# A seventh row pair in seven products, its sums T loaded apart for the first and last pair, and two low halves per block on GpSimd

## The chip, the cores and the metric

The kernel runs on one core of a Trainium2 chip. The core has a matrix engine (TensorE, PE in the profile), a vector engine (VectorE, DVE), a scalar engine (ScalarE, ACT), GpSimd (POOL) and SyncE (SP), which here only issues DMAs. The engines have queues of their own and meet at semaphores; matrix products land in PSUM, in eight banks of 128 x 512 fp32. The metric is the device time of one execution, in microseconds (us).

## The reference

Two pre-norm residual layers over 256 tokens of width 2048, each a token mixer (HGRN2 in layer 0, gated linear attention in layer 1) beside a cross-attention into 256 memory tokens, an output projection, and a SwiGLU feed-forward block with 5632 hidden columns. Everything is in fp32. The change is in the feed-forward part of both layers:

```python
hn = _rmsnorm(h, norm_ffn[layer])
gate, up = jnp.split(hn @ w_gate_up[layer], 2, axis=-1)
h = h + (jax.nn.silu(gate) * up) @ w_down[layer]
```

with `hn` of 256 x 2048, `w_gate_up` of 2048 x 11264 and `w_down` of 5632 x 2048.

## The kernel before

**Split factors.** A product of fp32 matrices is made as three matmuls of fp32r operands: each factor is split into a high part (a copy rounded to fp32r, by ACT) and a low part (the factor less its high part, by DVE), and high x high, high x low and low x high are summed in one PSUM bank. The low part of the weights is called the low half below; `split` makes both parts for one tile of raw weights.

**Blocks.** `ffn` goes over 11 blocks of 512 hidden columns. `up_block(b)` makes the 256 x 512 gate and up columns of block b with `project_halves`; a block reads 16 row tiles of 128 rows, taken as eight row pairs p = 0 to 7. Each pair has a 2 x 2 structure: two halves of the tokens by two row tiles on the left, two row tiles by two column groups (c0 for gate, c1 for up) on the right. There are three ways to make it, a letter for each pair in `KINDS`:

- S, seven products: the seven-product scheme for 2 x 2 matrices, in `seven`. It needs left forms s, d0, u, z and four combinations of the raw weights on the right, one of them T, the sum of the two row tiles in columns c1.
- O, eight products from the raw weights.
- H, eight products from the raw weights with one more difference of them (e1).

The string "SSOSSOSS", the last of `KINDS`, holds for blocks 4 to 10. The products go into seven PSUM banks, numbered 1 to 7, summed over the eight pairs; `TIMES` counts them.

**Raw weights.** `load_pair` loads the four tiles of a pair into one of three raw buffers (128 x 4 x 512) through SP's queue. For an S pair in the feed-forward part (`fed`), T is made by DMAs: SP loads the first row tile's c1 columns into place 1 of the raw buffer, and GpSimd issues a DMA that adds the second row tile's onto it. The second must wait for the first to land. The buffer is free when the last instruction that reads it is done. The split parts go into tiles a, b, c and d of the pair (`parts354c` is part c of the 354th raw tile); the larger ones share six buffers.

**Order.** From block 0's pair 3 on the order on PE, DVE and ACT is the program's (`Engine.kept`); GpSimd's and SP's are the scheduler's. Between the up blocks two pieces of the down projection run (`down`, tiles fd), each with one or two loads of 512 down weight rows (`weights`, two splits each). Work that belongs to block b but is done later is put down with a due key (`due`) and runs where `mark` passes it (`WHEN`): the sums of the seven banks (`sums`, tiles e and s), the gate (`gate`), the transposes (`turn`), and the copy of the finished down sums to h (`give_back`). From block 1 on the sums run right after the first down weights are split, and from block 3 on the copies to h run at the end of the second down load and at the second pair of the next block.

**The low half on GpSimd.** DVE's sums read one operand from PSUM. `sums` puts the name of its first addition into `free_port`; the next `split` takes it out, gives its low half to GpSimd, and makes it wait for that addition.

**Left forms.** `h_forms` makes the left factors of all pairs ahead of the block, eight forms for an S pair and six for an O pair (`Forms`, `PAIRS`).

Of the kernel before, what the change touches and what calls it, by code (L numbers as in the profile page):

```python
# [9 lines left out]
F32 = mybir.dt.float32  # L10
F32R = mybir.dt.float32r
BF16 = mybir.dt.bfloat16
U8 = mybir.dt.uint8
AF = mybir.ActivationFunctionType
ALU = mybir.AluOpType
AX = mybir.AxisListType

P = 128
T = 256
# [7 lines left out]
DFF = 5632  # L27
# [13 lines left out]
def trunk_kernel(ctx: ExitStack, tc: tile.TileContext, x, mem, norm_mix, norm_ffn, norm_mem,  # L41
                 norm_final, hgrn_w_in, hgrn_lb_logits, hgrn_onorm, gla_w_in, gla_w_gk,
                 gla_b_gk, gla_onorm, w_mem_kv, w_out, w_gate_up, w_down, c_ident, c_mask, out):
    nc = tc.nc

    const = ctx.enter_context(tc.tile_pool(name="const", bufs=1))
    wts = ctx.enter_context(tc.tile_pool(name="wts", bufs=1))
    away = ctx.enter_context(tc.tile_pool(name="away", bufs=1, space=bass.MemoryType.DRAM))
    opp = ctx.enter_context(tc.tile_pool(name="opp", bufs=8))
    work = ctx.enter_context(tc.tile_pool(name="work", bufs=1))  # L50
# [111 lines left out]
    pe, ve, ac = Engine(nc.tensor), Engine(nc.vector), Engine(nc.scalar)  # L162
# [102 lines left out]
    n_w = [0]  # L265
    free_port = []
# [8 lines left out]

    def split(src, name, by=2, turned=False):

        n, m = src.shape[1:]
        if n == 1:
            both = wts.tile([P, 2, 1, 512], F32R, tag="part", name=f"parts{name}", bufs=2)  # L280
        else:
            both = wts.tile([P, 2, 2, 512], F32R, tag="parts", name=f"parts{name}", bufs=6)
        for k in range(0, n, by):
            j = min(k + by, n)
            if turned:
                hi = both[:, 0, k:j, 0:m]
                ac.activation(out=hi, in_=src[:, k:j, :], func=AF.Copy, scale=-1.0)
                ve.scalar_tensor_tensor(out=both[:, 1, k:j, 0:m], in0=src[:, k:j, :], scalar=-1.0, in1=hi.bitcast(F32),
                                        op0=ALU.mult, op1=ALU.subtract)
                continue  # L290
            ac.copy(out=both[:, 0, k:j, 0:m], in_=src[:, k:j, :])
            low = (nc.gpsimd if free_port else ve).tensor_tensor(  # L292
                out=both[:, 1, k:j, 0:m], in0=src[:, k:j, :], in1=both[:, 0, k:j, 0:m].bitcast(F32), op=ALU.subtract)
            if free_port:
                tc.add_manual_dep(low.ins, free_port.pop(), mybir.DependencyInfo(
                    mybir.DependencyClass.Sync, mybir.DependencyReason.DATA), reason="port")
        return [(both[:, 0, k, 0:m], both[:, 1, k, 0:m]) for k in range(n)]

# [58 lines left out]

    PAIRS = "SSOSSOSB"  # L360
    HOMES = (("hq", "hq"),) * 4 + (("F", "K"), ("T", "sc"), ("Q", None), ("v", "gate"))
    FACTORS = {"S": ("x10", "x00", "x01", "x11", "s", "d0", "u", "z"), "O": ("x10", "x00", "x01", "x11", "d0", "d1"),
               "B": ("x10", "x00", "x01", "x11", "s", "d0", "u", "z", "d1")}
# [46 lines left out]

    TIMES = {"S": (1,) * 7, "O": (0, 2, 2, 2, 2, 0, 0), "H": (0, 2, 2, 2, 1, 0, 1)}

    def load_pair(raw, w, p, c0, c1, n, kind, fed):

        if n_w[0] == 1:
            for k, j, c in ((0, 0, c0), (0, 1, c1), (1, 3, c0), (1, 2, c1)):
                nc.sync.dma_start(out=raw[:, j, 0:n], in_=w[(2 * p + k) * P:(2 * p + k + 1) * P, c:c + n])
                if k == 0 and c == c1:
                    load_mem(0, 256, 512)
            return  # L420
        if kind == "S" and fed:
            rows = [w[(2 * p + k) * P:(2 * p + k + 1) * P, c1:c1 + n] for k in range(2)]
            nc.sync.dma_start(out=raw[:, 1, 0:n], in_=rows[0])
            nc.gpsimd.dma_start(out=raw[:, 1, 0:n], in_=rows[1], accum_op=ALU.add)  # L424
        nc.sync.dma_start(out=raw[:, 0:4:3, 0:n], in_=w[2 * p * P:(2 * p + 2) * P, c0:c0 + n].rearrange("(k p) c -> p k c", p=P))
        if kind == "S" and fed:
            nc.sync.dma_start(out=raw[:, 2, 0:n], in_=rows[1])
        else:
            nc.sync.dma_start(out=raw[:, 1:3, 0:n], in_=w[2 * p * P:(2 * p + 2) * P, c1:c1 + n].rearrange("(k p) c -> p k c", p=P))

    def seven(i, raw, fed, between=None):

        n = raw.shape[2]
        tt = ve.tensor_tensor
        b00, = split(raw[:, 0:1, :], f"{i}a")
        b11, b10 = split(raw[:, 2:4, :], f"{i}b")
        if between:
            between()

        if not fed:  # L440
            tt(out=raw[:, 1, :], in0=raw[:, 1, :], in1=raw[:, 2, :], op=ALU.add)
        tt(out=raw[:, 0, :], in0=raw[:, 1, :], in1=raw[:, 0, :], op=ALU.subtract)
        tt(out=raw[:, 2:4, :], in0=raw[:, 2:4, :], in1=raw[:, 0:1, :].broadcast_to([P, 2, n]), op=ALU.subtract)
        t6, t7 = split(raw[:, 0:2, :], f"{i}c", turned=True)
        t5, t4 = split(raw[:, 2:4, :], f"{i}d")
        return {1: ("x00", b00), 2: ("x01", b10), 3: ("z", b11), 4: ("x11", t4), 5: ("s", t5), 6: ("u", t6), 7: ("d0", t7)}

# [152 lines left out]
        for to, b in zip(out, (2, 4, 3, 8)):  # L600
            add(to, b, to)

    def project_halves(forms, kinds, w, c0, c1, name, key, keep):


        left = {b: sum(TIMES[kind][b - 1] for kind in kinds) for b in range(1, 8)}
        ps = {}

        def product(b, left_factor, right):
            first = b not in ps  # L610
            if first:
                ps[b] = bank(f"{name}p{b}")
            left[b] -= 1
            (xh, xl), (hi, lo) = left_factor, right
            pe.matmul(ps[b], xh, hi, start=first, stop=False)
            pe.matmul(ps[b], xh, lo, start=False, stop=False)
            pe.matmul(ps[b], xl, hi, start=False, stop=left[b] == 0)

        for p, kind in enumerate(kinds):
            Engine.kept = keep <= p  # L620
            i, raw = new_raw()
            fed = True
            load_pair(raw, w, p, c0, c1, 512, kind, fed)
            x = forms[p].get
            last = p == len(PAIRS) - 1
            if kind == "S":
                todo = seven(i, raw, fed, lambda: mark(key + p))
                for b in (1, 2, 6, 7, 5, 4, 3) if last else (1, 3, 2, 6, 7, 5, 4):
                    product(b, x(todo[b][0]), todo[b][1])
            else:  # L630
                b00, b01 = split(raw[:, 0:2, :], f"{i}a")
                mark(key + p)
                b11, b10 = split(raw[:, 2:4, :], f"{i}b")
                todo = [[(2, "x00", b00), (5, "x10", b01), (4, "x10", b00), (3, "d0", b01)]]
                if kind == "O":
                    todo.append([(2, "x01", b10), (5, "x11", b11), (4, "x11", b10), (3, "d1", b11)])
                else:
                    ve.tensor_tensor(out=raw[:, 3, :], in0=raw[:, 3, :], in1=raw[:, 2, :], op=ALU.subtract)
                    e1, = split(raw[:, 3:4, :], f"{i}c")
                    todo.append([(2, "x01", b10), (3, "x01", b11), (7, "x11", b11), (4, "x11", e1)])  # L640
                todo = [m for ms in zip(*todo) for m in ms] if last else todo[0] + todo[1]
                for b, f, right in todo:
                    product(b, x(f), right)
            step()
        return ps
# [525 lines left out]
    PARTS = ((0,), (1, 2), (3, 4), (5, 6), (7, 8), (9, 10))  # L1171


    KINDS = ("SHOSHOSO", "HHOSSOSO", "SHOSSOSO", "SSOSSOHS", "SSOSSOSS")

# [7 lines left out]
    def ffn(l, forms, r, after, tail=None):  # L1185
        sq = {}

        def up_block(b):
            ps = project_halves(forms, KINDS[min(b, 4)], w_gate_up[l], 512 * b, DFF + 512 * b, f"f{l}_{b}_",
                                100 * b, 0 if b else 3)  # L1190
            when = WHEN[min(b, 3)]
            got = {}

            def sums():
                got["e"] = e = work.tile([P, NT, 512], F32, tag="stg", name=f"e{l}_{b}", bufs=2)
                got["s"] = s = work.tile([P, NT, 512], F32, tag="stg", name=f"s{l}_{b}", bufs=2)
                e0, e1, s0, s1 = e[:, 0, :], e[:, 1, :], s[:, 0, :], s[:, 1, :]
                ac.copy(out=e0, in_=ps[1])
                for out, p, q in ((s0, 2, e0), (e1, 6, e0), (s1, 7, e1), (e1, 5, e1), (e0, 5, s1),
                                  (s1, 4, s1), (e1, 3, e1)):  # L1200
                    ve.tensor_tensor(out=out, in0=ps[p], in1=q, op=ALU.add)
                    if p == 2 and b:
                        free_port.append(ve.last)

            def gate():
# [39 lines left out]
        todo = []  # L1245
        for b in range(DFF // 512):
            up_block(b)
            todo += [(i, n) for i, part in enumerate(PARTS) if part[-1] == b - 1 for n in range(NQ)]
            for j in range(2):
                if todo:  # L1250
                    down(*todo.pop(0), 100 * b + 10 + 2 * j, 100 * b + WHEN[min(b, 3)]["back"][j])
# [4 lines left out]
        n = 0  # L1256
        made = []
        for plan in ENDS[l]:
# [4 lines left out]
            parts = []  # L1263
# [20 lines left out]
    scale = lambda ss=ss: h_scale(ss, "rx", True)  # L1284
    for l in range(2):
# [6 lines left out]
        turned = []  # L1292
# [12 lines left out]
        parts = []  # L1305
# [96 lines left out]
```

## Time and profile before

| what | value |
|---|---|
| time, median of three runs | 2261.01 us (2260.9 to 2262.21) |
| the profiled execution: time | 2261.07 us |
| the profiled execution: span from the first to the last instruction | 2259.0 us |
| granted TensorE clock, mean | 0.999 |
| mean DMA rate over the span | 210 GB/s |

The page of the profile gives each engine's busy time, the chain of work that ended last, and groups of instructions with count, busy time, mean duration, and the idle time ahead of them with what ended it. A row of the timeline gives start and duration in us, engine, line, operation, the tile written and the tiles read, shape, how many were merged, and in brackets the idle time of the engine before it and what ended it. Most instructions of DVE, ACT and PE have line L151, that of a helper, so they are told apart by tiles: f_p is the seven banks of an up block, fd the banks of the down projection, hf_2h the high left forms of pair 2.

Layer 0's feed-forward blocks run from about 516 to 1140 us, layer 1's from 1562 to 2185 us.

### The profile page before, as it was taken

Reading aid. Unit: us, or ns where it says so; the run is one execution under the profiler, and the core shown is the slowest. Engines: PE = TensorE matmul, PEld = TensorE weight load, DVE = VectorE, ACT = ScalarE, POOL = GpSimd, SP = SyncE. Lnnn points to the kernel's source line nnn. Section 1 sums busy time; section 2 is a strip of 40 time slices with the busy share of each in tenths; the row PEclk is TensorE's granted clock in tenths of the full one; section 3 lists DMA queues with packets and bytes.
Section 4 is the critical chain, followed back from the end, with each engine's and each line's share of the span. In section 5 each row is a group of like instructions: output and inputs, shape, how many; then the busy total and the mean of one; then the engine's idle time right before and its main releaser. Section 6 shows DMA issues by size and latency. Waiting matters only on the chain.

```text
span 2259.0 us, 30203 instructions
## 1 busy us (share of the span) xinstructions
PE 2245.2 (99%) x10710; PEld 1903.1 (84%) x10710; DVE 1974.4 (87%) x2459; ACT 1425.3 (63%) x1938; POOL 202.3 (9%) x205
## 2 busy tenths in 40 slices
PE   9999999999999999999999999999999999999998
PEld 7888888888888888888889999988888888888887
DVE  6889899898898989988986887889889898888987
ACT  7656656565666666665665665566566666666664
POOL 1000100000111111111100000000011111111110
PEclk9999999999999999999999999999999999999999
DMA  8656655665676777777765455566677777777774
GB/s 295 215 169 212 203 182 171 196 196 182 210 241 213 244 234 216 228 233 227 232 216 171 137 165 182 166 205 200 201 230 226 227 232 222 230 228 220 240 235 155
DMA packets 255691, 473.60 MB, mean 210 GB/s; under 512 B 17807, under 2 KB 47283, under 8 KB 255283
## 3 DMA queue, kind: packets, MB, share of 16 engines
q1 hardware_dynamic: 233507, 429.65, 56.8%
q0 software_dynamic: 20736, 37.76, 10.5%
q10 hardware_dynamic: 1296, 4.26, 0.5%
q8 instruction: 84, 1.38, 0.2%
q14 instruction: 68, 0.56, 0.1%
HBM read 468.45 MB, written 3.15 MB: 209 GB/s over the span
## 4 chain that ended last, share of the span: by engine, by line
PE 94%; DVE 2%; issue 1%; DMA 1%; ACT 0%; SPq 0%; POOLq 0%; DVEq 0%; POOL 0%; ACTq 0%
PE f_p L151 37%; PE fd L151 17%; PE wo L151 4%; PE m1p L151 2%; PE hv2p L151 2%; PE hv1p L151 2%; PE hv0p L151 2%; PE hf0p L151 2%; PE wo0p L151 2%; PE wo1p L151 2%; PE hf2p L151 2%; PE hf1p L151 2%; PE m0p L151 2%; PE gk0p L151 1%; PE gk1p L151 1%; PE gg11p L151 1%
## 5 line engine op out<-in xcount | busy, mean ns | idle before, releaser
L151 DVE TENSOR_TENSOR raw<-raw 128x512 f32<-128x512 f32 (+3 forms) x330 | 303.7, 921 | 49.8 <-DMA raw<-in_w_gate_up_dram 30.9
L151 ACT CAST parts<-raw 128x1024 fp32r<-128x1024 f32 (+1 forms) x216 | 212.2, 1017 | 48.5 <-PE gx L151 6.3
L151 DVE TENSOR_TENSOR parts<-raw,parts 128x1024 fp32r<-128x1024 f32 (+1 forms) x196 | 223.9, 1176 | 20.2 <-ACT parts L151 20.0
L424 POOL DMA_DIRECT2D raw<-in_w_gate_up_dram x114 | 98.8, 867 | 960.9 <-DMA raw<-in_w_gate_up_dram 348.6
L151 ACT COPY h<-fd 128x512 f32<-128x512 f32 x80 | 46.2, 588 | 84.6 <-PE fd L151 81.7
L292 POOL TENSOR_TENSOR parts<-raw,parts 128x1024 fp32r<-128x1024 f32 x20 | 48.7, 2433 | 232.6 <-ACT parts L151 219.0
L151 ACT ACTIVATE s<-s,rf_r 128x512 f32<-128x512 f32 x44 | 31.8, 723 | 44.0 <-DVE s L151 43.9
L151 DVE TENSOR_TENSOR e<-f_p,e 128x512 f32<-128x512 f32 x66 | 45.1, 684 | 2.3
L151 ACT COPY fd<-h 128x512 f32<-128x512 f32 x82 | 45.3, 585 | 0.0
L151 PE MATMUL fd<-parts,s_0h 128*128 128x512 f32 x128 | 39.8, 392 | 0.0
L151 PE MATMUL fd<-parts,s_8h 128*128 128x512 f32 x128 | 39.8, 392 | 0.0
L151 PE MATMUL fd<-parts,s_6h 128*128 128x512 f32 x128 | 39.8, 392 | 0.0
L151 PE MATMUL fd<-parts,s_4h 128*128 128x512 f32 x128 | 39.8, 392 | 0.0
L151 PE MATMUL fd<-parts,s_2h 128*128 128x512 f32 x128 | 39.8, 392 | 0.0
L151 PE MATMUL fd<-parts,s_5h 128*128 128x512 f32 x128 | 39.4, 389 | 0.0
L151 PE MATMUL fd<-parts,s_1h 128*128 128x512 f32 x128 | 39.4, 389 | 0.0
L151 PE MATMUL fd<-parts,s_7h 128*128 128x512 f32 x128 | 39.4, 389 | 0.0
L151 PE MATMUL fd<-parts,s_3h 128*128 128x512 f32 x128 | 39.4, 389 | 0.0
L151 DVE TENSOR_TENSOR s<-f_p,e 128x512 f32<-128x512 f32 x44 | 30.3, 688 | 10.0 <-PE f_p L151 8.1
L424 POOL DMA_DIRECT2D raw<-in_hgrn_w_in_dram x17 | 14.8, 874 | 210.8 <-DMA raw<-in_hgrn_w_in_dram 125.6
L151 DVE SCALAR_TENSOR_TENSOR s<-e,rf_r,s 128x512 f32<-128x512 f32 x44 | 31.0, 745 | 0.2
L151 PEld LDWEIGHTS fd<-parts,s_1h 128*128 128x128 f32 x128 | 24.0, 188 | 5.0
(5728 smaller groups left out, 7298.9 us busy)
## 6 DMA issues: line engine op xcount, KB each, us to landing
raw<-in_w_gate_up_dram SPq DMA_DIRECT2D x238, 512.0 KB, 4.8
raw<-in_w_down_dram SPq DMA_DIRECT2D x80, 1024.0 KB, 5.9
raw<-in_w_gate_up_dram SPq DMA_DIRECT2D x228, 256.0 KB, 4.0
raw<-in_hgrn_w_in_dram SPq DMA_DIRECT2D x79, 512.0 KB, 4.8
raw<-in_gla_w_in_dram SPq DMA_DIRECT2D x96, 384.0 KB, 3.9
raw<-in_w_gate_up_dram POOLq DMA_DIRECT2D x114, 256.0 KB, 5.3
raw<-in_w_out_dram SPq DMA_DIRECT2D x16, 1024.0 KB, 5.4
raw<-in_w_mem_kv_dram SPq DMA_DIRECT2D x27, 512.0 KB, 5.5
```

What stands on the lines that cost most here:

```text
L151: ins = func(*args, **kwargs)
L292: low = (nc.gpsimd if free_port else ve).tensor_tensor(out=both[:, 1, k:j, 0:m], in0=src[:, k:j, :], in1=both[:, 0, k:j, 0:m].bitcast(F32) ...
L424: nc.gpsimd.dma_start(out=raw[:, 1, 0:n], in_=rows[1], accum_op=ALU.add)
```

## The change

- Pair 2 gets the left forms of an S pair (`PAIRS`), and its kind goes from O to S in blocks 4 to 10 and from O to H in blocks 0 to 3 (`KINDS`).
- For pair 0, and for pair 7 where it is an S pair, T is made in a tile of its own (`load_apart`, tag "scx"), by two DMAs of GpSimd's queue, the second adding onto the first. For pair 0 of block b + 1 it is asked for after block b's last pair, ahead of the down projection; for pair 7 at pair 4. `seven` and `split` then take T from that tile, and the split of the two combinations T and T less the first tile is made in two steps of 512 columns each.
- `sums` puts two of its additions into `free_port` instead of one, and `split` takes the older first, so the next two splits give their low halves to GpSimd.

```diff
     def split(src, name, by=2, turned=False):
 
+        if isinstance(src, list):
+            both = wts.tile([P, 2, 2, 512], F32R, tag="parts", name=f"parts{name}", bufs=6)
+            for k in (1, 0):
+                hi = both[:, 0, k:k + 1, :]
+                ac.activation(out=hi, in_=src[k], func=AF.Copy, scale=-1.0)
+                ve.scalar_tensor_tensor(out=both[:, 1, k:k + 1, :], in0=src[k], scalar=-1.0, in1=hi.bitcast(F32),
+                                        op0=ALU.mult, op1=ALU.subtract)
+            return [(both[:, 0, k, :], both[:, 1, k, :]) for k in range(2)]
...
-                tc.add_manual_dep(low.ins, free_port.pop(), mybir.DependencyInfo(
+                tc.add_manual_dep(low.ins, free_port.pop(0), mybir.DependencyInfo(
...
-    PAIRS = "SSOSSOSB"
+    PAIRS = "SSSSSOSB"
...
+    def column(w, p, c1, n):
+        return [w[(2 * p + k) * P:(2 * p + k + 1) * P, c1:c1 + n] for k in range(2)]
+
+    def load_apart(w, p, c1):
+
+        both = work.tile([P, 1, 512], F32, tag="scx", name=f"T{n_w[0]}_{p}")
+        rows = column(w, p, c1, 512)
+        nc.gpsimd.dma_start(out=both[:, 0, :], in_=rows[0])
+        nc.gpsimd.dma_start(out=both[:, 0, :], in_=rows[1], accum_op=ALU.add)
+        return both
...
         if kind == "S" and fed:
-            rows = [w[(2 * p + k) * P:(2 * p + k + 1) * P, c1:c1 + n] for k in range(2)]
-            nc.sync.dma_start(out=raw[:, 1, 0:n], in_=rows[0])
-            nc.gpsimd.dma_start(out=raw[:, 1, 0:n], in_=rows[1], accum_op=ALU.add)
+            rows = column(w, p, c1, n)
+            if fed is True:
+                nc.sync.dma_start(out=raw[:, 1, 0:n], in_=rows[0])
+                nc.gpsimd.dma_start(out=raw[:, 1, 0:n], in_=rows[1], accum_op=ALU.add)
...
-        tt(out=raw[:, 0, :], in0=raw[:, 1, :], in1=raw[:, 0, :], op=ALU.subtract)
+        apart = fed if fed and fed is not True else None
+        tt(out=raw[:, 0, :], in0=apart[:, 0, :] if apart else raw[:, 1, :], in1=raw[:, 0, :], op=ALU.subtract)
         tt(out=raw[:, 2:4, :], in0=raw[:, 2:4, :], in1=raw[:, 0:1, :].broadcast_to([P, 2, n]), op=ALU.subtract)
-        t6, t7 = split(raw[:, 0:2, :], f"{i}c", turned=True)
+        t6, t7 = split([raw[:, 0:1, :], apart] if apart else raw[:, 0:2, :], f"{i}c", turned=True)
...
-            fed = True
+            if p == 4 and kinds[7] == "S":
+                apart[7] = load_apart(w, 7, c1)
+            fed = apart.get(p, True)
...
-    KINDS = ("SHOSHOSO", "HHOSSOSO", "SHOSSOSO", "SSOSSOHS", "SSOSSOSS")
+    KINDS = ("SHHSHOSO", "HHHSSOSO", "SHHSSOSO", "SSHSSOHS", "SSSSSOSS")
...
+        ready = {}
+
+        def first(b):
+            if KINDS[min(b, 4)][0] != "S":
+                return {}
+            return ready.pop(b, None) or {0: load_apart(w_gate_up[l], 0, DFF + 512 * b)}
+
         def up_block(b):
             ps = project_halves(forms, KINDS[min(b, 4)], w_gate_up[l], 512 * b, DFF + 512 * b, f"f{l}_{b}_",
-                                100 * b, 0 if b else 3)
+                                100 * b, 0 if b else 3, first(b))
...
-                    if p == 2 and b:
+                    if p in (2, 5) and out is not e0 and b:
                         free_port.append(ve.last)
...
         for b in range(DFF // 512):
             up_block(b)
+            if b + 1 < DFF // 512:
+                ready[b + 1] = first(b + 1)
```

More of the change, by code (lines that the diff above doesn't have):

```diff
@@ L601, in project_two, with project_halves @@
             add(to, b, to)
-    def project_halves(forms, kinds, w, c0, c1, name, key, keep):
+    def project_halves(forms, kinds, w, c0, c1, name, key, keep, apart):
         left = {b: sum(TIMES[kind][b - 1] for kind in kinds) for b in range(1, 8)}
```

## The prediction, made before the changed kernel ran

> **What bounds the kernel now.** I read the page's busy times and chain first. "Same" below means within 0.2%, 4.5 us, about what a measurement of this kernel can tell from no change.
>
> ```profile
> span 2259.0 us, 30203 instructions
> PE 2245.2 (99%) x10710; PEld 1903.1 (84%) x10710; DVE 1974.4 (87%) x2459; ACT 1425.3 (63%) x1938; POOL 202.3 (9%) x205
> PE 94%; DVE 2%; issue 1%; DMA 1%; ACT 0%; SPq 0%; POOLq 0%; DVEq 0%; POOL 0%; ACTq 0%
> ```
>
> The chain is TensorE for 94%: work taken from PE shortens the run, as long as nothing else becomes late. The change takes products from PE and gives work to DVE, so the question is DVE's room in the stage that is changed. The view by stretches for one late feed-forward block (length, busy time of PE, PEld, DVE, ACT and POOL with instructions, clock, DMA share, GB/s):
>
> ```profile
> 1871.78:1933.87 62.09, 62.09 (x279) 51.50 (x278) 56.24 (x59) 40.52 (x50) 7.61 (x7) 1.00 0.77 233
> ```
>
> PE has no hole in 62.09 us; DVE is idle 5.9 us. An average doesn't settle it, since PE takes each operand at a fixed place. So I read the timeline of this block, PE first: start, duration, and the split tile it reads (354 to 359 are row pairs 2 to 7).
>
> ```profile
> 1907.83 0.62 PE L151 MATMUL f_p<-parts354a,hf_2h 128*128 128x512 f32 x2
> 1913.27 0.62 PE L151 MATMUL f_p<-parts355a,hf_3h 128*128 128x512 f32 x2
> 1918.03 0.62 PE L151 MATMUL f_p<-parts356a,hf_4h 128*128 128x512 f32 x2
> 1920.07 0.62 PE L151 MATMUL f_p<-parts356c,hf_4h 128*128 128x512 f32 x2
> 1934.35 0.62 PE L151 MATMUL f_p<-parts359c,hf_7h 128*128 128x512 f32 x2
> 1937.75 0.62 PE L151 MATMUL fd<-parts,s_3h 128*128 128x512 f32 x2
> ```
>
> An O pair (2) holds PE for 1913.27 - 1907.83 = 5.44 us, an S pair (3) for 1918.03 - 1913.27 = 4.76: eight products or seven, **0.68 us each**. Then DVE in the same block:
>
> ```profile
> 1872.57 0.68 DVE L151 TENSOR_TENSOR s<-f_p,e 128x512 f32<-128x512 f32 x1
> 1877.35 1.22 DVE L151 TENSOR_TENSOR parts<-raw,parts 128x1024 fp32r<-128x1024 f32 x1
> 1878.48 1.41 DVE L151 SCALAR_TENSOR_TENSOR s<-e,rf_r,s 128x512 f32<-128x512 f32 x2
> 1879.81 4.62 DVE L151 TENSOR_TENSOR parts<-raw,parts 128x1024 fp32r<-128x1024 f32 x4
> 1887.93 0.69 DVE L151 TENSOR_TENSOR parts352a<-raw,parts352a 128x512 fp32r<-128x512 f32 x1 [3.50 <-ACT parts352a L151]
> 1900.14 1.23 DVE L151 SCALAR_TENSOR_TENSOR parts353c<-raw,parts353c 128x1024 fp32r<-128x1024 f32 x1 [0.97 <-ACT parts353c L151]
> 1902.42 1.22 DVE L151 TENSOR_TENSOR parts354a<-raw,parts354a 128x1024 fp32r<-128x1024 f32 x1
> 1904.69 0.68 DVE L151 TENSOR_TENSOR parts355a<-raw,parts355a 128x512 fp32r<-128x512 f32 x1
> 1910.71 0.68 DVE L151 TENSOR_TENSOR parts356a<-raw,parts356a 128x512 fp32r<-128x512 f32 x1
> 1914.40 1.22 DVE L151 SCALAR_TENSOR_TENSOR parts356c<-raw,parts356c 128x1024 fp32r<-128x1024 f32 x1
> 1928.86 1.23 DVE L151 SCALAR_TENSOR_TENSOR parts359c<-raw,parts359c 128x1024 fp32r<-128x1024 f32 x1
> 1931.60 2.60 DVE L151 TENSOR_TENSOR parts<-raw,parts 128x1024 fp32r<-128x1024 f32 x2 [0.33 <-ACT parts L151]
> 1934.62 0.69 DVE L151 TENSOR_TENSOR s<-f_p,e 128x512 f32<-128x512 f32 x1 [0.42 <-PE f_p L151]
> ```
>
> On DVE an O pair takes 1904.69 - 1902.42 = 2.27 us and an S pair 1910.71 - 1904.69 = 6.02. So DVE falls behind PE by 1.26 us in each S pair and gains 3.17 in each O pair. What it falls behind from is fixed in two places, where DVE waits (3.50 and 0.97 us) for ACT, and ACT for PE:
>
> ```profile
> 1886.11 1.27 ACT L151 COPY h<-fd 128x512 f32<-128x512 f32 x2 [3.68 <-PE fd L151]
> 1897.88 1.27 ACT L151 COPY h<-fd 128x512 f32<-128x512 f32 x2 [2.31 <-PE fd L151]
> 1930.51 1.05 ACT L151 CAST parts<-raw 128x1024 fp32r<-128x1024 f32 x1 [0.50 <-PE f_p L151]
> 1931.88 1.05 ACT L151 CAST parts<-raw 128x1024 fp32r<-128x1024 f32 x1 [0.32 <-PE f_p L151]
> 1933.87 0.59 ACT L151 COPY e<-f_p 128x512 f32<-128x512 f32 x1 [0.93 <-PE f_p L151]
> 1934.35 1.11 ACT L151 COPY fd<-h 128x512 f32<-128x512 f32 x2
> ```
>
> ACT gives the finished down projection back to h ahead of the casts of pair 0 and of pair 1's part c. So DVE can't start earlier, and its lead at pair 2 is what PE's own progress allows.
>
> **The change part by part.** *Pair 2 of blocks 4 to 10, 14 blocks in both layers, from O to S.* PE loses one product in each, three matmuls, 42 of 10710: 14 x 0.68 = **9.5 us**, all of it on the chain if PE never waits. DVE gets 6.02 - 2.27 = 3.75 us per block after the second fixed place. Lead in the tightest places, now and after (less 3.75, less the 0.68 by which PE arrives earlier): part c of pair 4 is ready at 1914.40 + 1.22 = 1915.62 and used at 1920.07, 4.45, after 0.02; part c of pair 7 is ready at 1930.09 and used at 1934.35, 4.26, after -0.17, and a few hundredths less for T's own half (below), -0.2. So PE waits some **0.2 us** per block. The next one late is ACT: its copies of h into the down banks (from 1934.35) follow the casts that follow DVE. They move by 3.75 less the waits ahead of them that close up, 0.50 + 0.32 + 0.93, so by 2.0; the first ends near 1936.9, and PE wants it at 1937.75 - 0.48 = 1937.3. That holds, by 0.4. Pair 2's own T is one transfer of 256 KB more per block, at a DMA share of 0.77, and its raw buffer is free from the down phase on, some 20 us ahead: nothing.
>
> *T of pairs 0 and 7 apart.* T (the sum of the right halves of the two row tiles) is an accumulating transfer. Into the raw buffer it can start only when that is free, and DVE waits for it at pair 7 of some blocks, here of the next one (the second row; the first is the same step of pair 6, without a wait; the third is every issue of GpSimd's):
>
> ```profile
> 1920.89 1.94 DVE L151 TENSOR_TENSOR raw<-raw 128x512 f32<-128x512 f32 x2
> 1990.70 1.95 DVE L151 TENSOR_TENSOR raw<-raw 128x512 f32<-128x512 f32 x2 [1.17 <-DMA raw<-in_w_gate_up_dram]
> DMA to landing us min/median/max: 3.9/5.0/8.6
> ```
>
> With T in its own tile and asked for at pair 4, that wait at pair 7 goes; if it stayed, the 0.2 above would be 1.4. The split of a pair with T apart runs in two halves of 512: by rows here 2 x 0.68 overlapped against 1.22, under 0.1 us more on DVE, and two casts on ACT, which has a third of its time free. Bytes are the same; SP loses one transfer, GpSimd's queue gets one, and in that queue the second one of a T stands waiting for the first. Where T is for the next block's pair 0, the two low halves stand behind it.
>
> *Two low halves on GpSimd.* One more low half leaves DVE, 1878.48 - 1877.35 = 1.13 us, and goes to GpSimd at 2.43:
>
> ```profile
> L292 POOL TENSOR_TENSOR parts<-raw,parts 128x1024 fp32r<-128x1024 f32 x20 | 48.7, 2433 | 232.6 <-ACT parts L151 219.0
> 1874.44 2.42 POOL L292 TENSOR_TENSOR parts<-raw,parts 128x1024 fp32r<-128x1024 f32 x1 [15.11 <-ACT parts L151]
> ```
>
> It lies in the down phase, where DVE is ahead. DVE reaches the sums 3.75 late less the 0.75 it idles there (0.33 + 0.42), at 1937.6; the 1872.57-to-1884.43 stretch up to the last down low half, 11.86, becomes 10.73: done at 1948.4, against the first fixed place 62.09 - 0.5 after 1887.93, 1949.5. So 1.1 us stay, and 0.97 behind it at the second. DVE's lateness doesn't pass from block to block unless some 2 us are added.
>
> What the second GpSimd half costs DVE, no row shows: today's (1874.44 to 1876.86) lies beside the sums, which read one operand from PSUM; the second would run on, 0.7 to 2.4 us, beside the gate and low halves, with both inputs in SBUF. Nearest rows: nothing (the sums keep 0.68) and its whole 2.4. I take 0.7, what sticks out of the sums if both halves follow at once; it fits the 1.1. The Trainium skill, "SBUF — State Buffer", section "Who interferes with whom", says that a VectorE instruction with two SBUF inputs and a GpSimd one that reads SBUF exclude each other for a whole instruction; by it DVE would stand still for up to 2.4 us per block, 0.3 more than the 1.1 + 0.97, and the sum below would be 1.6 instead of 6.2. No row shows the two side by side.
>
> *Pair 2 of blocks 0 to 3 from O to H.* As many products, but DVE makes a difference and one more low half, waiting for ACT between. Rows of an H pair (block 1, pair 1), and the tightest place behind it, on DVE and on PE:
>
> ```profile
> 562.88 1.22 DVE L151 TENSOR_TENSOR parts93b<-raw,parts93b 128x1024 fp32r<-128x1024 f32 x1
> 566.46 1.23 DVE L151 TENSOR_TENSOR parts94a<-raw,parts94a 128x1024 fp32r<-128x1024 f32 x1 [0.26 <-ACT parts94a L151]
> 579.45 1.22 DVE L151 SCALAR_TENSOR_TENSOR parts96c<-raw,parts96c 128x1024 fp32r<-128x1024 f32 x1
> 582.86 0.62 PE L151 MATMUL f_p<-parts96c,hf_4h 128*128 128x512 f32 x2
> ```
>
> From b to the next pair 566.46 - 562.88 = 3.58 instead of 1.13 us: 2.45 more. The lead at 96c, 582.86 - 580.67 = 2.19, becomes -0.26: 0.3 in block 1 of each layer, 0.5 in all. Blocks 0, 2 and 3 I put at nothing, since block 0 has no down projection beside its pairs and block 3 loses a wait at pair 7; as much as in block 1, 0.3 in each of six, is kept for the range. Two more left forms of pair 2, about 1 us of DVE per layer, hide behind the output projection.
>
> **Sum:** 14 x (0.68 - 0.2) = 6.7, less 0.5: 6.2 us. From the profiled execution's own 2261.07 (span 2259.0 and 2.1 around it; the median shown is 2261.01): **2254.9 us**.
>
> **The rivals.**
> 1. *Nothing is late* (chance 0.1). If PE never waits, 9.5 us go: 2251.5. For it: DVE's total fits. Against: leads of 0.02 and -0.2 leave no room.
> 2. *The gain goes to DVE* (0.25). Pair 7's T above waited 1.17 us though its raw buffer was freed an S pair, an O pair and two low halves before, 6.02 + 2.27 + 1.8 = 10.1 us. Pair 6 now is the last with T in a raw buffer, at the same distance. A third of that wait, 0.35, leaves 14 x (0.68 - 0.55) - 0.5 = 1.3: **2260**; all of it makes the change slower. Against: pair 6 has this distance already (1910.71 to 1920.89) and shows no wait.
> 3. *GpSimd's queue* (0.22; the slower side). T for the next block is asked for when DVE has used pair 7's, near 1933.9; it lands 5.0 us later by the median, then the accumulating issue takes 0.87, and the two low halves end at 1942.2 and 1944.6. PE needs them at 1942.9 and 1945.6. From a landing of 6.2 on PE waits 0.5 more and the gain is gone; at 7.2, within the 8.6 shown, it waits 1.5: 14 x (0.68 - 1.7) - 0.5 = -15, **2276**, and both halves then lie wholly beside DVE's gate and low halves. For it: 1 MB weight loads run at that moment. Against: the queue may put the low halves first.
>
> **How the numbers follow.** The forecast has 0.43. Its own 2251 to 2258 reaches over the 0.2% line (2256.5), as 0.12 us per block more does that, so a part of it counts as same. Faster: 0.35 of the forecast and rival 1's 0.1, 0.45. Same: the rest, 0.08, and most of rival 2, 0.30. Slower: rival 3 and the worse end of rival 2, 0.25. The range: 2251, all hidden, to 2271, which leaves out the upper part of rival 3.
>
> **What would show it.** PE with 10668 matmuls and pair 2's tiles a to d in blocks 4 to 10. Right: PE idle of a few tenths ahead of parts c of pairs 4 and 7, released by DVE, no DVE wait for DMA at pair 7, 40 low halves on GpSimd. Wrong: PE waiting in fd for GpSimd (rival 3), DVE waiting for DMA at pair 6 (rival 2), DVE operations of twice their length beside GpSimd's low halves, or a later DVE start at pair 0 than ACT's return of h.

## The result, and the profile after

| | before | after |
|---|---|---|
| median, eight runs each on one chip | 2261.13 us (2260.45 to 2262.58) | 2254.74 us (2253.52 to 2256.62) |
| the profiled execution: time | 2261.07 us | 2254.6 us |
| its span | 2259.0 us | 2252.8 us |

The ratio of the medians is 0.9971, with a 95% interval of 0.9961 to 0.998: 6.4 us faster. The forecast was 2254.9.

From the page of the changed kernel come the span, the busy times, the shares of the chain, and two groups of instructions, GpSimd's low halves and DVE's gate:

```profile
span 2252.8 us, 30400 instructions
PE 2238.6 (99%) x10668; PEld 1894.6 (84%) x10668; DVE 2031.5 (90%) x2551; ACT 1452.8 (64%) x2010; POOL 280.4 (12%) x275
PE 90%; DVE 6%; issue 2%; DMA 1%; ACT 1%; SPq 0%; POOL 0%; DVEq 0%; POOLq 0%; ACTq 0%
L300 POOL TENSOR_TENSOR parts<-raw,parts 128x1024 fp32r<-128x1024 f32 x40 | 95.6, 2406 | 113.5 <-ACT parts L151 81.2
L151 DVE SCALAR_TENSOR_TENSOR s<-e,rf_r,s 128x512 f32<-128x512 f32 x44 | 45.7, 1076 | 2.9 <-ACT s L151 0.5
```

PE has the 42 matmuls less that the change takes out, and GpSimd does 40 low halves. DVE's share of the chain goes from 2% to 6%: by the rows below, PE now meets DVE's results with nothing to spare. The last row is the gate; it was 745 ns (31.0 us over 44), and is 1076.

Where the time went is read from the view by stretches, cut at PE's first product of blocks 0 and 4, its last product of block 10, and the same three in the second layer. The columns are the stretch, its length, and the busy time of PE, PEld, DVE, ACT and POOL, then clock, DMA share and GB/s. Before:

```profile
516.27:728.34 212.07, 212.07 (x957) 175.79 (x955) 186.58 (x209) 133.98 (x170) 22.28 (x21) 1.00 0.71 220
728.34:1140.11 411.77, 411.77 (x1842) 341.49 (x1841) 369.51 (x384) 267.13 (x326) 49.42 (x47) 1.00 0.76 227
1140.11:1562.06 421.95, 420.26 (x2340) 386.64 (x2338) 350.82 (x548) 263.24 (x412) 16.54 (x25) 1.00 0.57 179
1562.06:1774.12 212.06, 212.06 (x956) 175.79 (x955) 186.69 (x209) 134.06 (x170) 21.76 (x21) 1.00 0.71 219
1774.12:2185.90 411.78, 411.78 (x1843) 341.49 (x1841) 369.79 (x385) 267.44 (x326) 49.54 (x47) 1.00 0.76 228
```

After:

```profile
516.76:729.66 212.90, 212.55 (x956) 175.58 (x955) 192.06 (x218) 136.63 (x178) 31.51 (x28) 1.00 0.71 218
729.66:1137.05 407.39, 407.39 (x1821) 337.55 (x1820) 390.21 (x416) 276.62 (x350) 73.99 (x69) 1.00 0.80 231
1137.05:1560.03 422.98, 420.38 (x2339) 386.71 (x2338) 352.76 (x553) 264.58 (x415) 22.00 (x29) 1.00 0.56 181
1560.03:1772.90 212.87, 212.75 (x957) 175.58 (x955) 192.98 (x218) 136.52 (x178) 31.55 (x28) 1.00 0.71 218
1772.90:2180.49 407.59, 407.59 (x1822) 337.45 (x1820) 390.10 (x416) 276.68 (x350) 73.91 (x69) 1.00 0.80 231
```

- **Blocks 4 to 10**: 411.77 to 407.39 and 411.78 to 407.59, 8.6 us less in the two layers. PE has 21 matmuls less in each and, at this resolution, no idle time.
- **Blocks 0 to 3**: 212.07 to 212.90 and 212.06 to 212.87, 1.6 us more.
- **Between** (end of layer 0, the mixer of layer 1): 1.0 us more in this pair of executions, of which 0.9 is PE's idle time (421.95 - 420.26 against 422.98 - 420.38). The stretch ahead of the first block adds 0.5.

The same kernel before, profiled again, has the two kinds of FFN stretches to the hundredth (212.07 and 411.77) but 517.2 ahead of them and 421.0 between. The changed kernel, profiled again (run 9), has 407.28 and 407.64 us in blocks 4 to 10, but 213.61 and 213.29 in blocks 0 to 3, 2.8 us more than before instead of 1.6. So blocks 4 to 10 can be compared to about 0.1 us, the stretches in which PE waits only to about 1 us.

In the late block whose timeline the prediction showed (block 6 of layer 1), DVE after the change:

```profile
1874.51 0.69 DVE L151 TENSOR_TENSOR s<-f_p,e 128x512 f32<-128x512 f32 x1
1878.10 2.01 DVE L151 SCALAR_TENSOR_TENSOR s<-e,rf_r,s 128x512 f32<-128x512 f32 x2
1883.36 2.36 DVE L151 TENSOR_TENSOR parts<-raw,parts 128x1024 fp32r<-128x1024 f32 x2 [0.97 <-ACT parts L151]
1885.79 0.69 DVE L151 TENSOR_TENSOR parts352a<-raw,parts352a 128x512 fp32r<-128x512 f32 x1
1897.66 1.23 DVE L151 SCALAR_TENSOR_TENSOR parts353c<-raw,parts353c 128x1024 fp32r<-128x1024 f32 x1 [0.61 <-ACT parts353c L151]
1911.11 1.23 DVE L151 TENSOR_TENSOR parts355d<-raw,parts355d 128x1024 fp32r<-128x1024 f32 x1 [0.24 <-ACT parts355d L151]
1915.94 1.22 DVE L151 SCALAR_TENSOR_TENSOR parts356c<-raw,parts356c 128x1024 fp32r<-128x1024 f32 x1
1922.29 1.95 DVE L151 TENSOR_TENSOR raw<-raw 128x512 f32<-128x512 f32 x2
1928.30 0.69 DVE L151 TENSOR_TENSOR raw<-T,raw 128x512 f32<-128x512 f32 x1
1930.77 0.69 DVE L151 SCALAR_TENSOR_TENSOR parts359c<-raw,parts359c 128x512 fp32r<-128x512 f32 x1
```

and PE at the two tight places:

```profile
1916.91 0.81 PE L151 MATMUL f_p<-parts356c,hf_4h 128*128 128x512 f32 x2
...
1931.41 0.62 PE L151 MATMUL f_p<-parts359c,hf_7h 128*128 128x512 f32 x2
```

The first fixed place (352a, where DVE waited 3.50 us) is used up: its row has no bracket any more, and a wait of 0.97 at the down weights stands ahead of it instead. The second (353c) still waits, 0.61. Behind it DVE waits once more in this block, 0.24 us for ACT at part d of pair 3 (355d). Part c of pair 4 is done at 1915.94 + 1.22 = 1917.16 and PE comes for it at 1916.91, so its two matmuls take 0.81 us instead of 0.62: the wait, 0.2 us. Part c of pair 7 is done at 1930.77 + 0.69 = 1931.46 as PE begins on it, at 1931.41, without a stretched row. Pair 6 (1922.29) and pair 7 (1928.30) don't wait for their T.

This block is not like the others. From its first product to that of the next block PE takes 61.69 us, in the other blocks 4 to 9 of both layers 61.45 to 61.49 (62.09 before), and no other block from 4 on has DVE's wait at pair 3 in this execution. In the other thirteen, part c of pair 4 is done 0.01 to 0.02 us ahead of PE and part c of pair 7 0.02 to 0.06 ahead. In the block before this one, DVE and then PE, each from its timeline (344 is pair 4):

```profile
1854.20 1.22 DVE L151 SCALAR_TENSOR_TENSOR parts344c<-raw,parts344c 128x1024 fp32r<-128x1024 f32 x1
```

```profile
1855.44 0.63 PE L151 MATMUL f_p<-parts344c,hf_4h 128*128 128x512 f32 x2
```

Part c is done at 1855.42, 0.02 us ahead of PE. What delays ACT's cast of 355d in block 6 is not known. The wait is there again in runs 6, 7 and 9.

GpSimd at the start of the same block:

```profile
1869.42 0.57 POOL L428 DMA_DIRECT2D T<-in_w_gate_up_dram  x1 [14.70 <-DVE parts347c L151]
1872.74 0.86 POOL L429 DMA_DIRECT2D T<-in_w_gate_up_dram  x1 [2.75 <-DMA T<-in_w_gate_up_dram]
1874.13 4.77 POOL L300 TENSOR_TENSOR parts<-raw,parts 128x1024 fp32r<-128x1024 f32 x2 [0.53 <-ACT parts L151]
```

T's two transfers do stand ahead of the low halves in GpSimd's queue. But the first has landed by 1872.74 - 1869.42 = 3.3 us after its issue (2.8 to 3.1 us from issue to landing for pair 0 of every block from 4 to 10, in both layers), and what the low halves then wait for is ACT, 0.5 us.

### The profile page after: what moved, and what is told of

Its sections match the earlier page's. It is cut to its first block, busy times and chain, and to the rows that moved or that the text cites. A ratio compares the mean times of both kernels' runs of the same rounds, so it can differ in the third digit from the quotient of the medians.

```text
span 2252.8 us, 30400 instructions
## 1 busy us (share of the span) xinstructions
PE 2238.6 (99%) x10668; PEld 1894.6 (84%) x10668; DVE 2031.5 (90%) x2551; ACT 1452.8 (64%) x2010; POOL 280.4 (12%) x275
## 4 chain that ended last, share of the span: by engine, by line
PE 90%; DVE 6%; issue 2%; DMA 1%; ACT 1%; SPq 0%; POOL 0%; DVEq 0%; POOLq 0%; ACTq 0%
PE f_p L151 34%; PE fd L151 18%; PE wo L151 4%; PE m1p L151 2%; PE hv2p L151 2%; PE hv1p L151 2%; PE hf0p L151 2%; PE hv0p L151 2%; PE wo1p L151 2%; PE hf2p L151 2%; PE hf1p L151 2%; PE wo0p L151 2%; PE m0p L151 2%; PE gk0p L151 1%; PE gk1p L151 1%
## 5 line engine op out<-in xcount | busy, mean ns | idle before, releaser
L151 DVE TENSOR_TENSOR raw<-raw 128x1024 f32<-128x1024 f32 (+3 forms) x330 | 311.2, 943 | 16.7 <-DMA raw<-in_w_down_dram 5.6
L151 DVE TENSOR_TENSOR parts<-raw,parts 128x1024 fp32r<-128x1024 f32 (+1 forms) x176 | 200.2, 1171 | 22.7 <-ACT parts L151 22.0
L444 POOL DMA_DIRECT2D raw<-in_w_gate_up_dram x92 | 80.4, 873 | 541.2 <-DMA raw<-in_w_gate_up_dram 274.7
L300 POOL TENSOR_TENSOR parts<-raw,parts 128x1024 fp32r<-128x1024 f32 x40 | 95.6, 2406 | 113.5 <-ACT parts L151 81.2
L428 POOL DMA_DIRECT2D T<-in_w_gate_up_dram x36 | 21.1, 587 | 430.2 <-DVE hf_4g L151 82.7
L151 DVE SCALAR_TENSOR_TENSOR s<-e,rf_r,s 128x512 f32<-128x512 f32 x44 | 45.7, 1076 | 2.9 <-ACT s L151 0.5
L429 POOL DMA_DIRECT2D T<-in_w_gate_up_dram x36 | 31.0, 861 | 120.4 <-DMA T<-in_w_gate_up_dram 111.1
```

The source lines that it names most:

```text
L151: ins = func(*args, **kwargs)
L300: low = (nc.gpsimd if free_port else ve).tensor_tensor(out=both[:, 1, k:j, 0:m], in0=src[:, k:j, :], in1=both[:, 0, k:j, 0:m].bitcast(F32) ...
L428: nc.gpsimd.dma_start(out=both[:, 0, :], in_=rows[0])
L429: nc.gpsimd.dma_start(out=both[:, 0, :], in_=rows[1], accum_op=ALU.add)
```

## The experiments

Two theories were to be told apart. *Mine*: DVE's lead behind the second fixed place bounds the blocks, the loads made ahead hold it, and the second GpSimd half lies in a stretch with time to spare. *The rival*: the low half on GpSimd, one more taken from DVE, is what makes room. A question of its own was what the H pair costs in blocks 0 to 3. Unless something else is said, the diffs are against the changed kernel; ratios are against the kernel before on the same chip, and stretches are those of the view above.

**1. T apart and two low halves, with the old kinds of pairs.**

```diff
-    PAIRS = "SSSSSOSB"
+    PAIRS = "SSOSSOSB"
...
-    KINDS = ("SHHSHOSO", "HHHSSOSO", "SHHSSOSO", "SSHSSOHS", "SSSSSOSS")
+    KINDS = ("SHOSHOSO", "HHOSSOSO", "SHOSSOSO", "SSOSSOHS", "SSOSSOSS")
```

> T apart and two low halves on GpSimd stay, pair 2 goes back to O in every block (left forms too). Theory (the gain is the product that PE saves, and nothing else of the change makes PE faster): PE has its 10710 matmuls again and had no hole before, so 2261, within 0.2% of the kernel before. Rival (the T tile and the two low halves give some of the gain by themselves, since DVE's waits at pair 7 go): 2258 or less.

Measured: 2264.92 us against 2262.1, ratio 1.0015 (1.0006 to 1.0024). It was expected to be even, and is 2.8 us slower. The blocks are not the reason: they have the lengths of before in both layers (212.07 and 411.77). (The profiled execution took 2266.6 us, so its stretches show more than the 2.8.) The stretch between them has changed:

```profile
1142.28:1566.69 424.41, 420.38 (x2339) 386.65 (x2338) 350.83 (x546) 263.00 (x412) 20.54 (x29) 1.00 0.56 176
```

PE is idle for 4.0 us of it, 1.7 before. The view of waits for PE at the end of layer 0, 1140 to 1215 us (who waited for whom, total, times, longest), says where:

```profile
PE fd_0p L151 <- DVE parts210c L151: 1.7, 1, 1.7
PE tp_hm L151 <- DVE h L151: 1.0, 2, 0.8
```

These are the last pieces of the down projection and the transposes of h behind them; the kernel before has 0.2 us of the second wait and none of the first. So, by itself, what was meant to make room wins nothing and costs a little, outside the blocks.

**2. One low half on GpSimd instead of two.**

```diff
-                    if p in (2, 5) and out is not e0 and b:
+                    if p == 2 and b:
```

> The changed kernel with one low half per block on GpSimd instead of two. Theory: DVE gets 1.13 us of low half back and loses the 0.65 us by which the gate's first operation is drawn out beside the second half (1.37 us in the changed kernel, 0.72 before); the 0.5 that stays is taken up at the second fixed place, where DVE waits 0.6: 2254.7, within 0.1%. Rival (DVE's work in the down phase is passed on to the pairs): 14 x 0.5 = 7 us more, 2261.7.

Measured: 2256.98 us, ratio 0.9978 (0.9969 to 0.9987), which is not told apart from the changed kernel's 0.9971 (0.9961 to 0.998). Blocks 4 to 10 of layer 0:

```profile
731.26:1138.69 407.43, 407.43 (x1821) 337.67 (x1820) 392.80 (x422) 276.81 (x350) 59.99 (x63) 1.00 0.81 231
```

407.43, and 407.51 in the other layer, against 407.39 and 407.59: in the blocks that the change is about, the second low half is worth nothing. The 2.6 us that DVE does more here (392.80 against 390.21) lie in the down phase, ahead of both fixed places. The rival falls.

**3. T of pair 7 in the raw buffer again.**

```diff
-            if p == 4 and kinds[7] == "S":
+            if p == 4 and kinds[7] == "-":
```

> The changed kernel with pair 7's T in the raw buffer as before; pair 0's stays apart. Theory: DVE's lead at pair 7's part c is 0.05 us in the changed kernel, so the wait for T there (1.2 to 2 us in the kernel before) reaches PE in full: 14 blocks x 1.2 to 1.9 = 17 to 27 us, 2272 to 2281, PE idle ahead of part c of pair 7. Rival (DVE comes later now, so T is there in time): 2255.

Measured: 2269.52 us, ratio 1.0034 (1.0022 to 1.0046), 2.5 us below the band that was expected. DVE at pair 7 of a late block, then PE's row that waits for it, each from its timeline:

```profile
888.49 1.95 DVE L151 TENSOR_TENSOR raw<-raw 128x512 f32<-128x512 f32 x2 [1.05 <-DMA raw<-in_w_gate_up_dram]
```

```profile
891.72 0.50 PE L151 MATMUL f_p<-parts155c,hf_7h 128*128 128x512 f32 x1 [0.76 <-DVE parts155c L151]
```

Blocks 4 to 10 take 415.05 and 414.40 us instead of 407.39 and 407.59: some 1.0 us more per block. That eats the 0.68 and more: without T apart the seventh seven-product pair makes the kernel slower than before.

**4. Pair 2 as an O pair in blocks 0 to 3, an S pair in the others.** The O pair needs one left form (d1) beside those of an S pair; it and pair 5's low forms share a tile.

```diff
-    PAIRS = "SSSSSOSB"
+    PAIRS = "SSDSSOSB"
...
+                "D": ("x10", "x00", "x01", "x11", "s", "d0", "u", "z")}
...
+            if self.kind == "D":
+                tt(out=g[:, 4, :], in0=g[:, 2, :], in1=g[:, 3, :], op=ALU.subtract)
+                ac.copy(out=self.d1[:, 0, :], in_=g[:, 4, :])
+                tt(out=self.d1[:, 1, :], in0=g[:, 4, :], in1=self.d1[:, 0, :].bitcast(F32), op=ALU.subtract)
...
-    KINDS = ("SHHSHOSO", "HHHSSOSO", "SHHSSOSO", "SSHSSOHS", "SSSSSOSS")
+    KINDS = ("SHOSHOSO", "HHOSSOSO", "SHOSSOSO", "SSOSSOHS", "SSSSSOSS")
```

> The changed kernel with pair 2 as O in blocks 0 to 3, as before, and S in blocks 4 to 10; its left forms get d1 besides, in the unused part of a tile of pair 5. Theory: the PE waits in blocks 0 to 2 of the changed kernel (0.3 + 0.7 in layer 0, 0.45 + 0.2 in layer 1 by its timeline) come from the H pairs and go: 1.6 us less, 2253.1, no PE idle ahead of part c in block 1. Rival (they come from elsewhere, or the form d1 costs as much): 2254.7.

Measured: 2254.91 us (five runs, 2252.6 to 2255.21) against 2262.1, ratio 0.9962 (0.9949 to 0.9976). The expected 2253.1 was reckoned from the first measurements, where the kernel before takes 2261.1; as a ratio it is 0.9964, and that was met. Blocks 0 to 3 have their old length again, in both layers:

```profile
520.12:732.19 212.07, 212.07 (x957) 175.84 (x955) 187.60 (x210) 134.59 (x174) 32.10 (x28) 1.00 0.74 222
```

So all that blocks 0 to 3 lost is the H pair's.

**5. T of pair 0 in the raw buffer again.**

```diff
-            if KINDS[min(b, 4)][0] != "S":
+            if KINDS[min(b, 4)][0] != "-":
```

> The changed kernel with pair 0's T in the raw buffer as before; pair 7's stays apart. Theory: that buffer is freed by GpSimd's second low half, some 5 us later than DVE freed it before (1878.9 in the changed kernel's block), and T needs about 10 us from there, so it is ready near 1889.5 where DVE asks for it at 1887.9; 0.6 of the 1.6 is taken up at the second fixed place: 14 x 1.0 = 14 us more, 2269. Rival (the wait is covered, pair 0's lead is 7 us): 2255.

Measured: 2273.83 us against 2261.26, ratio 1.0054 (1.0039 to 1.0069), 4.8 us more than was expected. DVE now waits for T at pair 0 (part 148 is pair 0 of block 6):

```profile
851.58 1.95 DVE L151 TENSOR_TENSOR raw<-raw 128x512 f32<-128x512 f32 x2 [1.76 <-DMA raw<-in_w_gate_up_dram]
```

This comes between the two fixed places, and is more than the 0.61 that was left at the second. In the blocks where DVE waits, the wait is 1.2 to 4.1 us. PE waits 0.6 to 0.8 us ahead of part c of pair 4 in each of blocks 5 to 10 of this layer, and blocks 4 to 10 take 417.89 and 415.48 us.

**6. The second low half begun later, beside the gate.** It is made to wait for the last of the seven additions instead of the fourth.

```diff
-                    if p in (2, 5) and out is not e0 and b:
+                    if (p == 2 or p == 3) and b:
```

> The changed kernel with the second low half made to wait for the last of the seven sums instead of the fourth addition, so that it lies wholly beside DVE's gate and low halves, whose inputs are both in SBUF. Theory (a GpSimd low half and such a DVE operation exclude each other for a whole instruction): a DVE operation there grows by up to 2.4 us, against 0.65 now; of the 1.75 more 0.9 is taken up at the two fixed places: 14 x 0.9 = 12 us more, 2267. Rival (they only share a port now and then): gate operations of 0.7 to 1 us and 2254.7.

Measured: 2257.4 us, ratio 0.9982 (0.9973 to 0.9991), against an expected 2267. In the same block as above, GpSimd and then DVE:

```profile
1876.47 2.41 POOL L300 TENSOR_TENSOR parts<-raw,parts 128x1024 fp32r<-128x1024 f32 x1 [0.57 <-ACT parts L151]
1880.47 2.41 POOL L300 TENSOR_TENSOR parts<-raw,parts 128x1024 fp32r<-128x1024 f32 x1 [1.59 <-DVE e L151]
```

```profile
1880.44 3.65 DVE L151 SCALAR_TENSOR_TENSOR s<-e,rf_r,s 128x512 f32<-128x512 f32 x2
1900.00 1.23 DVE L151 SCALAR_TENSOR_TENSOR parts353c<-raw,parts353c 128x1024 fp32r<-128x1024 f32 x1 [0.55 <-ACT parts353c L151]
```

Two gate operations, 1.41 us in the kernel before, take 3.65, so DVE stood still for 2.24 us of GpSimd's 2.41. GpSimd's own time is the same. The trace agrees with the Trainium skill ("SBUF — State Buffer", section "Who interferes with whom"), by which a VectorE instruction with two SBUF inputs and a GpSimd one that reads SBUF exclude each other. But the price that I had put on it isn't paid: at 353c DVE still waits 0.55 us for ACT, 0.61 without the standstill, and blocks 4 to 10 take 407.43 and 407.59. The wait of 0.97 at the down weights and smaller ones behind it have closed up. My expectation had DVE's room there too small.

**7. One more DVE operation ahead of pair 2**, in blocks 4 to 10, behind the second fixed place (it makes a tile that nobody reads).

```diff
+                if p == 2 and kinds[2] == "S":
+                    extra = work.tile([P, 512], BF16, tag="junk", name=f"extra{i}")
+                    ve.tensor_tensor(out=extra, in0=h[:, 0, 0:512], in1=h[:, 0, 0:512], op=ALU.add)
```

> The changed kernel with one more DVE addition of 128 x 512, 0.6 us, ahead of pair 2 where it is an S pair (14 blocks); its result is not used. Theory (DVE's lead is used up to 0.02 at pair 4 and 0.05 at pair 7, so anything more on DVE behind the second fixed place is PE's wait): 14 x 0.58 = 8 us more, 2263. Rival (DVE isn't the limit there, PE keeps its pace): 2254.7.

Measured: 2262.66 us, ratio 1.0008 (0.9998 to 1.0018), as expected (2263). The operation starts 0.60 us ahead of the next one (DVE's timeline):

```profile
1904.56 0.68 DVE L151 TENSOR_TENSOR extra<-h 128x512 bf16<-128x512 f32 x1
1905.16 0.69 DVE L151 TENSOR_TENSOR parts354a<-raw,parts354a 128x512 fp32r<-128x512 f32 x1
```

and blocks 4 to 10 grow by 3.9 us in each layer, 411.24 and 411.51, which is 0.55 per block. Nine tenths of each us that DVE gets there is PE's too: the lead is used up. Put ahead of both fixed places, 2.24 us had cost nothing (run 6). This pair of runs is what shows where the bound is.

**8 to 11. Before, the changed kernel, run 4 and run 1 again.** The last three shared a chip and its runs of the kernel before (2262.24 us).

> The kernel before, unchanged, for a second profile. Theory: 2261 and PE's starts within 0.3 us of the first profile from stage to stage. What differs by more between two profiles of one kernel can't be put down to the change: above all the 0.9 us that the changed kernel lost at the end of layer 0's down projection.

> The changed kernel once more, beside the next two on one chip. Theory: 0.997 of the kernel before; by PE's starts 212.9 us for blocks 0 to 3 and 407.4 to 407.6 for blocks 4 to 10 of each layer, as in its first profile (212.1 and 411.8 before), while the time up to the first feed-forward block differs by a us or more from execution to execution.

> Pair 2 as O in blocks 0 to 3 and S in blocks 4 to 10, beside the changed kernel on one chip. Theory: 1.6 us below the changed kernel in the medians, since its blocks 0 to 3 take 212.1 instead of 212.9 us in each layer and all else is the same. Rival (the left form d1 or something outside the blocks takes it back): no difference, 0.997 of the kernel before.

> T apart and two low halves with the kinds of before, on another chip. It came out 0.15% over the kernel before, with blocks of the same length to a hundredth. Theory (that loss lies outside the blocks, at the end of layer 0's feed-forward part where PE waited 1.7 us for a T in a raw buffer): 1.001 to 1.002 again and a PE wait of 1 us or more there again. Rival (it was a chance of that execution): 1.000 and no wait there.

| kernel | median, us | ratio and interval |
|---|---|---|
| before again, one execution on the chip of runs 5 to 7 | 2261.09 | |
| changed, again | 2255.32 | 0.997 (0.9957 to 0.9982) |
| O in blocks 0 to 3, again | 2253.29 | 0.9963 (0.9951 to 0.9976) |
| old kinds, T apart and two low halves, again | 2265.18 | 1.0013 (1.0004 to 1.0022) |

Two of the expectations failed in part. The kernel before repeats its feed-forward blocks to a hundredth of a us, but the stretches ahead of them and between them differ by 0.9 us each, where 0.3 was expected. The changed kernel again has blocks 4 to 10 within about 0.1 us of the expected length, but blocks 0 to 3 take 213.61 and 213.29 us instead of 212.9. In block 1 of layer 0 PE now waits for pair 3 as well as for pair 4:

```profile
580.50 0.50 PE L151 MATMUL f_p<-parts95c,hf_3h 128*128 128x512 f32 x1 [0.44 <-DVE parts95c L151]
586.45 0.51 PE L151 MATMUL f_p<-parts96c,hf_4h 128*128 128x512 f32 x1 [0.39 <-DVE parts96c L151]
```

The version with O in blocks 0 to 3 is 2.0 us below the changed kernel on the same chip, where 1.6 was expected; the feed-forward stretches of these two executions give 2.1. It has the old length of blocks 0 to 3 in both of its executions and both layers (212.06 or 212.07). The intervals of the two ratios overlap, so that it beats the changed kernel rests on these stretches and on medians that agree. One of its blocks, block 5 of layer 1 in run 10, takes 62.05 us instead of 61.47, because DVE waits there for pair 3's T:

```profile
1845.04 1.95 DVE L151 TENSOR_TENSOR raw<-raw 128x512 f32<-128x512 f32 x2 [0.58 <-DMA raw<-in_w_gate_up_dram]
```

So a T that lands late behind the second fixed place costs PE about the whole of DVE's wait. That is what rival 2 feared, here at another pair and in one block. This version beats the kernel before by 0.37%.

The loss of run 1 came again, 2.9 us, but not with the same wait. The stretch in this execution:

```profile
1141.35:1564.33 422.98, 420.36 (x2339) 386.60 (x2338) 350.67 (x546) 263.21 (x412) 20.60 (x29) 1.00 0.56 177
```

PE is idle for 2.6 us of it, and waits 0.2 instead of 1.7 for part 210c, where 1 or more was expected; the 1.0 us for h is the same. In both executions, and not in the kernel before, DVE waits 0.7 us for ACT ahead of part 210b and 0.7 ahead of s_20m, a left form of the last down products. From the last product of block 10 to PE's last of all, 65.95 us go by instead of 65.20 (66.23 in run 1, but also 65.80 in the changed kernel again). So the loss is of the same size on two chips and lies outside the blocks, by these profiles at the end of both layers for the greater part; what in the two edits brings it was not settled.

## Why the prediction was right, and where it was not

The mechanism was right. That the total was right to a fraction of a us is in part luck: two terms were too small, with opposite signs, and the rest of the kernel is not as still as the sum supposed.

1. *One product per block, 9.5 us, 42 matmuls.* Right: 10710 to 10668.
2. *The fixed places.* Right, and the ground of the whole argument: DVE's time ahead of them costs nothing as long as the waits there can take it up (runs 2 and 6; run 5's wait of 1.76 was too long for the 0.61 left at the second), and behind the second one nine tenths of it is PE's (run 7).
3. *PE waits 0.2 us per block, so 6.7 us remain.* The mechanism was right, the size was not: **the blocks won 8.6 us**, 0.61 each, so PE loses 0.07 per block to waits and not 0.2. The lead of 0.02 at pair 4 was met to a hundredth in thirteen of fourteen blocks. The term that was mis-sized is the lead of -0.2 at pair 7: it is 0.02 to 0.06 in these thirteen, and -0.05 in the block shown, where DVE comes late from pair 3 and PE has already waited at pair 4. The lead was worked out with DVE's time from pair 4 to pair 7 in the kernel before, 1930.09 - 1915.62 = 14.47, which in the changed kernel is 1931.46 - 1917.16 = 14.30. It held a small wait, between these two rows of the kernel before:

```profile
1916.73 1.22 DVE L151 TENSOR_TENSOR parts357a<-raw,parts357a 128x1024 fp32r<-128x1024 f32 x1
1918.01 1.23 DVE L151 TENSOR_TENSOR parts357b<-raw,parts357b 128x1024 fp32r<-128x1024 f32 x1
```

From one to the next it is 1.28 us here and 1.13 in the changed kernel (1918.28 and 1919.41): a DVE that runs later doesn't wait there. And T's split in two steps, put at a few hundredths, cost nothing: from the first of pair 7's combinations to the end of part c it is 3.16 us (1928.30 to 1931.46), 3.18 before (1926.91 to 1930.09).
4. *T apart for pair 7; if its wait stayed, 1.4 instead of 0.2.* Right: run 3 put it back, and DVE waited 1.05, and a block took 1.0 us more.
5. *The H pair in blocks 0 to 3, 0.5 us in all.* Too small: **1.6 us** in this execution, 1.2 in those of runs 2, 3 and 6, which have the same H pairs, 2.0 in run 7's and 2.8 in the changed kernel's second (run 9). By PE's starts, block 1 lost 0.69 and 0.41 in the two layers where 0.3 was put (1.41 and 1.10 in run 9); block 0 lost 0.15 and 0.18 and block 2 of one layer 0.21, where nothing was put. The 0.3 for each of six blocks that was kept for the range would have been nearer. What makes it 1.2 in one execution and 2.8 in another is open. In the end of block 1 of layer 0 (timeline of PE, then DVE, changed kernel):

```profile
584.26 0.50 PE L151 MATMUL f_p<-parts96c,hf_4h 128*128 128x512 f32 x1 [0.35 <-DVE parts96c L151]
```

```profile
571.96 0.69 DVE L151 TENSOR_TENSOR parts94c<-raw,parts94c 128x512 fp32r<-128x512 f32 x1 [0.77 <-ACT parts94c L151]
572.57 0.69 DVE L151 TENSOR_TENSOR parts95a<-raw,parts95a 128x512 fp32r<-128x512 f32 x1
```

The place is the one that was named, part c of pair 4, and DVE's wait for ACT between the difference and its low half is in the rows.

6. *The second low half, 0.7 us of DVE's standstill, within a bound of 2.4.* Right in size: the gate takes 2.01 us instead of 1.41, 0.6 more, as GpSimd's second half (1874.13 + 4.77 = 1878.90) reaches into it. One of the signs named for being wrong is there, the gate's first operation at twice its length (1.35 us of the 2.01), and yet it is no loss. It costs nothing, and nearly the whole of the bound, in run 6, cost nothing either. The sum that the prediction set beside it, by which a standstill of 2.4 us leaves 1.6 us of the gain, went wrong in the room: more than the 1.1 + 0.97 us that it allowed closed up.
7. *The rivals.* GpSimd's queue: the order was as feared, but T's first transfer landed in about 3 us, not the 6.2 from which it would have decided, and PE shows no wait for GpSimd in the blocks. The gain going to DVE: pair 6 shows no wait for its T in any block from 4 on, and run 10 had one such wait, at pair 3. Nothing late: no, but nearer than thought, since 8.6 of 9.5 us arrived.

Blocks alone: -8.57 + 1.64 = -6.93 us, forecast -6.2. The two stretches ahead of the FFN parts took 1.5 back (0.5 and 1.0) and the end, from PE's last product on, gave 0.8, so the span fell by 6.2. Whether the change has a part in the 1.0 at the end of layer 0 is open: the changed kernel profiled again has 422.00 there and run 4's two executions 421.58 and 421.67, against 421.95 and 421.03 of the kernel before. The two more left forms of pair 2, which the prediction put at nothing, lie in these two stretches too; differences of 0.9 us between executions of one kernel hide what they cost.

## What to carry to other kernels

Find the places where the engine that follows is set by the leader's own progress, and weigh the work by where it lies: here a microsecond was free ahead of them, as far as the waits there could take it up, and cost 0.9 behind the last. Then look at more than one block: the one that was worked out, and shown again, was the one in fourteen with a wait of its own. Loads made ahead showed no gain of their own (run 1) and were still what made the change possible (runs 3 and 5), so a part that is worth nothing alone is to be tried by taking it away from the whole. A term put at nothing "because there is room" is to be worked out block by block: a few small ones cost 1.2 to 2.8 us where 0.5 was put, of the 9.5 that the products could give, and run 4 got it back.

## What the runs showed of the hardware that was not expected

The gate's DVE operations, which have both inputs in SBUF, stood still for nearly as long as GpSimd's low half was under way: 2.24 us of a 2.41 us operation in run 6, with GpSimd's time unchanged. DVE's sums, with one input in PSUM, keep their length beside GpSimd's low halves: the sum at 1874.51 above takes 0.69 us with GpSimd at work from 1874.13 on.

The kernel before repeats to a hundredth of a us, in two executions, in the stretches that PE fills (212.07 and 411.77), and differs by 0.9 us in those where it doesn't: 516.27 and 517.2 us ahead of the first block. The changed kernel, where PE just meets DVE, differs by 0.1 us in blocks 4 to 10 (407.39 and 407.28), and by 0.7 in blocks 0 to 3 of layer 0, where PE waits (212.90 and 213.61).
